# The last store of a rotary-embedding kernel: 128 partitions in one transfer, or 127 and then one in pieces

## The chip, the cores and the metric

The kernel runs on one core of a Trainium2 chip. The metric is device time in microseconds (us) of one execution; the time before is the median of three runs. Engines are named as in the profile: PE is TensorE, DVE is VectorE, ACT is ScalarE, POOL is GpSimd, SP is SyncE. SyncE and ScalarE issue the transfers; 16 DMA engines carry them out.

## The reference

The input is `x` of 16 batches x 512 positions x 1024 values in float32, 32 MiB, seen as 16 heads of 64. `cos` and `sin` are 512 x 32. Each head's two halves are rotated:

```python
x = x.reshape(batch, seq, num_heads, head_dim)
x1, x2 = (x[..., :half_dim].copy(), x[..., half_dim:].copy())
cos = cos[None, :, None, :].copy()
sin = sin[None, :, None, :].copy()
rotated = np.concatenate([x1 * cos - x2 * sin, x1 * sin + x2 * cos], axis=-1)
```

The output has the size of the input, so 32 MiB are read and 32 MiB written at the least.

## The kernel before

**Tiles.** The 16 batches make ten tiles (L41). Batches 0, 1, 14 and 15 are tiles of their own ("singles"): each of 128 partitions holds `R1` = 4 consecutive positions, one run of 4 x 1024 float32 = 16 KB in DRAM and in SBUF. The other twelve batches go in pairs: a partition holds `R2` = 8 consecutive positions of one batch, a run of 32 KB, and the two batches of a pair alternate over the partitions. A position of all 128 partitions is one unit of work `u` (128 x 1024 values); there are `NU` = 64. All tiles live in one ring in SBUF, `x_sb`, of 40 units; the result is written over the input.

**The work of a unit.** `on_vector` multiplies x by cos into PSUM (L332), `on_gpsimd` multiplies the swapped halves by the signed sin (L292; for some units VectorE does it, L325), and the sum is either VectorE's (`comb`, L343) or, for the units of `PE2`, an accumulation on TensorE (L253) that ScalarE copies back to SBUF (L220).

**Loads.** `on_scalar` issues most loads (L155), `on_sync` those of tile 2 and half of tile 0 (L162). The last three loads wait for a store to free their part of the ring (`later`, `sem_out`).

**Stores.** `on_sync` goes through the units; at the last unit of a tile `wait_added` waits until its sums are in SBUF, and one `dma_start` writes the tile. `in_sbuf(t)` gives the tile as 128 partitions x the run of a partition, `in_dram(o1, o2, t)` the same bytes in DRAM. Stores whose space a load needs count on their own semaphore `sem_out[k]`; the rest, among them the last, count on `sem_rest`, each by 16. After the last store SyncE waits until `sem_rest` has counted them all, and the program ends. All stores, in order, are on SyncE's queue (q1 in the profile); ScalarE's is q10.

The last tile is batch 15, a single: 128 rows of 16 KB, 2 MiB.

Of the kernel before, what the change touches and what calls it, by code (L numbers as in the profile page):

```python
# [6 lines left out]
def bass_split_heads_rope_kernel(  # L7
# [22 lines left out]
    R2 = 2 * R1  # L30
# [11 lines left out]
    NT = len(tiles)  # L42
# [3 lines left out]
    NU = len(rows)  # L46
    EARLY = (NU - RING) // R2
# [20 lines left out]
    EH = H * HD // BANK  # L68
    LEAD = 1
    LAG = 14  # L70

    with ExitStack() as stack:
        x_sb = stack.enter_context(nc.sbuf_tensor([P, RING, H, 2, HALF], fp32))
# [13 lines left out]
        sem_rest = stack.enter_context(nc.semaphore("rest"))  # L87
# [22 lines left out]
        o1 = out.rearrange("b (s r) h d -> b s (r h d)", r=R1)  # L110
        x2 = x.rearrange("b (s r) d -> s b (r d)", r=R2)
        o2 = out.rearrange("b (s r) h d -> s b (r h d)", r=R2)
        xs = x_sb[:].rearrange("p n h t d -> p n (h t d)")

        def in_dram(single, pairs, t):
            b, n = tiles[t]
            return single[b] if n == R1 else pairs[:, b:b + 2, :]

        def in_sbuf(t):
            b, n = tiles[t]  # L120
            k = b * R1 % RING
            return x_sb[:, k:k + n].rearrange("p n h t d -> p (n h t d)")

        def where(u):
            t, r = rows[u]
            return t, r, u % RING
# [7 lines left out]
        def wait_added(eng, u):  # L134

            if n_pe[u]:
                eng.wait_ge(sem_a, n_pe[u])
            if n_comb[u]:
                eng.wait_ge(sem_v, n_comb[u])
# [10 lines left out]
        def stores_of(k):  # L150

            return sum(b * R1 // R2 == k for b, _ in tiles)
# [4 lines left out]
        def load_rows(eng, t, lo, hi, sem):  # L157
            w = x.shape[2]
            src = in_dram(x1, x2, t)
            src = src[:, lo * w:hi * w] if tiles[t][1] == R1 else src[:, :, lo * w:hi * w]  # L160
            k = tiles[t][0] * R1 % RING
            eng.dma_start(  # L162
                x_sb[:, k + lo:k + hi].rearrange("p n h t d -> p (n h t d)"), src
            ).then_inc(sem, 16)

        def load_table(eng, i):
            table, sem = ((cos, sem_cos), (sin, sem_sin))[i]
            eng.dma_start(stage[:, i, :], table.rearrange("(s r) d -> s (r d)", r=R1)).then_inc(sem, 16)  # L168
# [9 lines left out]
        def on_sync(sp):  # L178
            load_rows(sp, 0, R1 // 2, R1, sem_in[0])
            load_table(sp, 1)  # L180
            load_rows(sp, 2, 0, R1, sem_in[2])
            load_rows(sp, 2, R1, R2, sem_low)
            for u in range(NU):
                t, r, k = where(u)
                if r == tiles[t][1] - 1:
                    wait_added(sp, u)
                    k = u // R2
                    sp.dma_start(in_dram(o1, o2, t), in_sbuf(t)).then_inc(sem_out[k] if k < EARLY else sem_rest, 16)
            sp.wait_ge(sem_rest, 16 * sum(stores_of(k) for k in range(EARLY, NU // R2)))

        def on_scalar(ae):
            later = {}
            for t, (b, n) in enumerate(tiles):
# [7 lines left out]
                else:  # L201

                    later.setdefault((b * R1 - RING) // R2 * R2 + R2 - 1 + LAG, []).append(t)

# [94 lines left out]
        def on_vector(ve):  # L299
# [50 lines left out]
            for u in range(NU + LEAD):  # L350
                if u < NU:
                    mul(u)
                if u >= LEAD and not PE2[u - LEAD]:
                    comb(u - LEAD)

        on_sync(nc.sync)
        on_scalar(nc.scalar)
        on_gpsimd(nc.gpsimd)
# [35 lines left out]
```

## Time and profile before

| | |
|---|---|
| time, median of three runs | 161.31 us (161.28 to 161.55) |
| the profiled execution: time, span | 161.29 us, 159.9 us |
| granted TensorE clock, mean | 0.795 |
| busy share of the span: DVE, POOL, PE, ACT | 81%, 82%, 40%, 15% |
| DMA packets, bytes, mean rate | 3457, 67.25 MB, 421 GB/s |
| SyncE's queue q1, ScalarE's queue q10, share of 16 engines | 57.0%, 41.5% |
| store of a single, issue to landing, median of four | 23.1 us |
| store of a pair, issue to landing, median of six | 32.2 us |
| the last store, issue and landing | issued at 146.97 us, landed 12.9 us later |

The span runs from the first to the last instruction of the profiled execution. The page cuts it into 40 equal slices; a digit is the busy share of a slice in tenths, for an engine or as a mean over the 16 DMA engines. The DMA view can be asked for any stretch of time; it then cuts that stretch into 40 slices, puts each packet into the slice in which it starts, and counts the packets by size. Here a packet of 16 KB is one partition's row of a single, one of 32 KB is a row of a pair, one of 512 B is a row of a table, and the tiny ones under 512 B are the writes with which an engine reports that its part of a transfer is done. "Share of 16 engines" is the packets' time over 16 times the stretch.

### The profile page before, as it was taken

The numbers are of one execution on the slowest core, as the hardware profiler recorded it, in microseconds if no ns is written. First come the engines' busy times: TensorE is split into PE (matmuls) and PEld (weight loads), VectorE is DVE, ScalarE is ACT, GpSimd is POOL, SyncE is SP. The second block draws the span as 40 slices with busy tenths as digits, with TensorE's granted clock in tenths as the row PEclk, the third lists the DMA queues.
The fourth block names the chain that finished last, engine by engine and source line by source line (L and its number), as shares of the span: only waits on it lengthen the run. The fifth ranks groups of instructions, "written<-read, shape, count | busy, mean of one in ns | idle before, by whom it ended". The sixth has DMA issues, their size and how long they took to land.

```text
span 159.9 us, 503 instructions
## 1 busy us (share of the span) xinstructions
PE 63.9 (40%) x94; PEld 21.6 (14%) x94; DVE 129.5 (81%) x117; ACT 24.4 (15%) x27; POOL 131.5 (82%) x41
## 2 busy tenths in 40 slices
PE   6050008076408640887076407640887075000000
PEld 1020011021102110222021102110222021000000
DVE  0069777999999999998999999999998995497000
ACT  0420001103300430024003300430024005000000
POOL 1069999999999999999999999999999981991000
PEclk9999999999985899557659975899557959855555
DMA  5999999999999999999999999999999999999896
GB/s 137 417 446 435 430 447 476 394 394 418 435 492 426 396 410 443 484 426 402 435 476 402 394 517 394 402 455 394 459 439 467 439 422 443 410 402 492 353 455 275
DMA packets 3457, 67.25 MB, mean 421 GB/s; under 512 B 384, under 2 KB 640, under 8 KB 640
## 3 DMA queue, kind: packets, MB, share of 16 engines
q1 hardware_dynamic: 2016, 38.86, 57.0%
q10 hardware_dynamic: 1440, 28.38, 41.5%
q14 instruction: 1, 0.01, 0.0%
HBM read 33.69 MB, written 33.55 MB: 421 GB/s over the span
## 4 chain that ended last, share of the span: by engine, by line
DMA 55%; DVE 19%; POOL 6%; issue 6%; PE 3%; ACT 1%; ACTq 1%; DVEq 0%; SPq 0%
DMA x_sb<-in_x_dram 34%; DMA out_dram<-x_sb 22%; DVE t_ps L332 9%; DVE x_sb L343 8%; POOL t_sb L292 6%; PE t_ps L253 3%; DVE t_sb L325 2%; ACT x_sb L220 1%; ACTq L168 0%; ACTq L162 0%; ACTq L155 0%; DVE tab_ps L309 0%; DVEq L342 0%; DVE tab_ps L310 0%; DVEq L329 0%
## 5 line engine op out<-in xcount | busy, mean ns | idle before, releaser
L292 POOL TENSOR_TENSOR t_sb<-x_sb,s_sb 128x2048 f32<-128x2048 f32 (+1 forms) x35 | 130.8, 3785 | 12.3 <-ACT s_sb L212 8.2
L253 PE MATMUL t_ps<-t_sb,ident 128*128 128x512 f32 x84 | 59.1, 847 | 63.9 <-DVE t_ps L332 51.6
L332 DVE TENSOR_TENSOR t_ps<-x_sb,pair_ps 128x1024 f32<-128x1024 f32 x48 | 57.5, 1220 | 0.8 <-ACT x_sb L220 0.8
L343 DVE TENSOR_TENSOR x_sb<-t_ps,t_sb 128x1024 f32<-128x1024 f32 x43 | 52.2, 1216 | 4.6 <-POOL t_sb L292 4.4
L220 ACT ACTIVATE x_sb<-t_ps 128x1024 f32<-128x1024 f32 x21 | 21.5, 1023 | 101.9 <-PE t_ps L253 101.9
L253 PEld LDWEIGHTS t_ps<-t_sb,ident 128*128 128x128 f32 x84 | 19.7, 260 | 103.1 <-DVE t_ps L332 74.0
L332 DVE TENSOR_TENSOR t_ps<-x_sb,tab_ps 128x1024 f32<-128x1024 f32 x16 | 19.2, 1222 | 3.0 <-ACT x_sb L220 2.0
L325 DVE TENSOR_TENSOR t_sb<-x_sb,tab_ps 128x1024 f32<-128x1024 f32 x6 | 7.3, 1210 | 0.0
L302 DVE COPY tab_ps<-stage 128x128 f32<-128x128 f32 x1 | 0.3, 294 | 8.0 <-DMA stage<-in_cos_dram 8.0
L237 PE MATMUL pair_ps<-stage,pick 128*128 128x256 f32 x4 | 2.0, 664 | 5.3 <-DMA stage<-in_cos_dram 5.3
L230 PE MATMUL t_ps<-zero 128*128 128x512 bf16 x6 | 2.7, 630 | 1.2 <-DVE zero L300 1.2
L237 PEld LDWEIGHTS pair_ps<-stage,pick 128*128 128x128 f32 x4 | 1.2, 322 | 6.3 <-issue 6.1
L206 ACT ACT_TABLE_LOAD x1 | 1.3, 1283 | 4.2 <-issue 4.2
L230 PEld LDWEIGHTS t_ps<-zero 128*128 128x128 bf16 x6 | 0.7, 138 | 2.3 <-DVE zero L300 1.2
L300 DVE MEMSET zero<- 128x256 uint32 x1 | 0.3, 272 | 0.9 <-PEq L376 0.9
L211 ACT ACTIVATE s_sb<-stage 128x128 f32<-128x128 f32 x1 | 0.3, 309 | 3.0 <-DMA stage<-in_sin_dram 3.0
L215 ACT ACTIVATE s_sb<-pair_ps 128x256 f32<-128x256 f32 x1 | 0.4, 384 | 1.9 <-PE pair_ps L237 1.9
L264 POOL MEMSET ident<- 128x128 f32 x1 | 0.2, 205 | 0.3 <-POOLq L376 0.3
L206 ACT ACTIVATE pick<-ident 128x256 f32<-128x256 f32 x1 | 0.4, 416 | 0.0
L216 ACT ACTIVATE s_sb<-pair_ps 128x256 f32<-128x256 f32 x1 | 0.4, 378 | 0.0
L266 POOL TENSOR_SCALAR_AFFINE_SELECT ident<-ident 128x128 f32<-128x128 f32 x1 | 0.3, 292 | 0.1
L376 POOL MEMSET const-float32-0.0<- 128x1 f32 x1 | 0.1, 98 | 0.3 <-issue 0.3
(6 smaller groups left out, 1.0 us busy)
## 6 DMA issues: line engine op xcount, KB each, us to landing
out_dram<-x_sb SPq DMA_DIRECT2D x6, 4096.0 KB, 32.2
x_sb<-in_x_dram ACTq DMA_DIRECT2D x5, 4096.0 KB, 31.3
out_dram<-x_sb SPq DMA_DIRECT2D x4, 2048.0 KB, 23.1
x_sb<-in_x_dram ACTq DMA_DIRECT2D x3, 2048.0 KB, 22.7
x_sb<-in_x_dram SPq DMA_DIRECT2D x2, 2048.0 KB, 23.9
x_sb<-in_x_dram SPq DMA_DIRECT2D x1, 1024.0 KB, 7.5
x_sb<-in_x_dram ACTq DMA_DIRECT2D x1, 1024.0 KB, 7.9
stage<-in_sin_dram SPq DMA_DIRECT2D x1, 64.0 KB, 7.7
```

Of the source, the lines that this page charges most:

```text
L206: ae.activation(pick[:], ident[:].rearrange("q (s k) -> q k s", k=2)[:, :, :, None].broadcast_to([P, 2, P // 2, 2]), COPY).then_inc(sem_g, 1)
L211: ae.activation(s1_sb[:, :, 0, :], sv, COPY, scale=-1.0)
L215: ae.activation(s2[:, :, :, 0, :], pair_ps[:, :, 1, :, :], COPY, scale=-1.0)
L216: ae.activation(s2[:, :, :, 1, :], pair_ps[:, :, 1, :, :], COPY).then_inc(sem_s, 1)
L220: ae.activation(xs[:, u % RING, :], t1_ps[:, u % NT1, :], COPY).then_inc(sem_a, 1)
L230: pe.matmul(t1_ps[:, k, b * BANK:(b + 1) * BANK], zero[:, 0:P], zero[:], start=True, stop=True).then_inc(sem_w, 1)
L237: pe.matmul(pair_ps[:, k].rearrange("p c r d -> p (c r d)"), pick[:, k].rearrange("q s b -> q (s b)"), stage[:].rearrange("q c f -> q (c f)"),
L253: ins = pe.matmul(t1_ps[:, u % NT1, b * BANK:(b + 1) * BANK], ident[:], t2[:, b * BANK:(b + 1) * BANK], start=False, stop=True, skip_group ...
L292: pl.tensor_tensor(t2_sb[:, u % NT2:u % NT2 + n], x_sb[:, k:k + n, :, ::-1, :], table[:, :, None, :, :].broadcast_to([P, n, H, 2, HALF]), ...
L325: ve.tensor_tensor(t2_sb[:, u % NT2, :, :, :], swapped(k), over_heads(v_ps), mult)
L332: ve.tensor_tensor(t1_ps[:, u % NT1, :].rearrange("p (h d) -> p h d", d=HALF), x_sb[:, k, :, :, :].rearrange("p h t d -> p (h t) d"), c_of ...
L343: ve.tensor_tensor(xs[:, k, :], t1_ps[:, u % NT1, :], t2_sb[:, u % NT2, :, :, :].rearrange("p h t d -> p (h t d)"), add,).then_inc(sem_v, 1)
```

## The change

The last tile's store is taken out of the common line and goes through a new function `store_last`, still on SyncE's queue and at the same place in its order. It issues three transfers: partitions 0 to 126 as they were, and partition 127, whose run of 16 KB is seen as 32 pieces of 512 bytes, in two transfers of 16 pieces each (the even pieces, then the odd ones). All three count on `sem_rest`, so the last wait asks for 32 more. No other store, load or computation is touched.

```diff
+    WHOLE = 127
+    PIECE = 128
...
                     k = u // R2
+                    if t == NT - 1:
+                        store_last(sp, t)
+                        continue
                     sp.dma_start(in_dram(o1, o2, t), in_sbuf(t)).then_inc(sem_out[k] if k < EARLY else sem_rest, 16)
-            sp.wait_ge(sem_rest, 16 * sum(stores_of(k) for k in range(EARLY, NU // R2)))
+            sp.wait_ge(sem_rest, 16 * (2 + sum(stores_of(k) for k in range(EARLY, NU // R2))))
+
+        def store_last(sp, t):
+
+            dst, src = in_dram(o1, o2, t), in_sbuf(t)
+            sp.dma_start(dst[:WHOLE], src[:WHOLE]).then_inc(sem_rest, 16)
+            for i in range(2):
+                piece = [a[WHOLE:].rearrange("p (q i e) -> p q i e", i=2, e=PIECE)[:, :, i, :] for a in (dst, src)]
+                sp.dma_start(*piece).then_inc(sem_rest, 16)
```

## The prediction

> **What bounds the kernel now.** I read the page's slices and queue list first, then the chain, SyncE's waits, the DMA issues, and last the DMA view over short windows at the end. The page and its DMA part:
>
> ```profile
> span 159.9 us, 503 instructions
> ...
> DMA  5999999999999999999999999999999999999896
> GB/s 137 417 446 435 430 447 476 394 394 418 435 492 426 396 410 443 484 426 402 435 476 402 394 517 394 402 455 394 459 439 467 439 422 443 410 402 492 353 455 275
> DMA packets 3457, 67.25 MB, mean 421 GB/s; under 512 B 384, under 2 KB 640, under 8 KB 640
> ...
> q1 hardware_dynamic: 2016, 38.86, 57.0%
> q10 hardware_dynamic: 1440, 28.38, 41.5%
> ...
> DMA 55%; DVE 19%; POOL 6%; issue 6%; PE 3%; ACT 1%; ACTq 1%; DVEq 0%; SPq 0%
> ```
>
> The 16 DMA engines are busy in every slice but the first and the last ones: 57.0 + 41.5 = 98.5% of the span, and DMA holds 55% of the chain. VectorE (81%) and GpSimd (82%) have slack. SyncE's waits, and its last issue in the timeline:
>
> ```profile
> SPq L189 <- DMA out_dram<-x_sb: 12.5, 1, 12.5
> ...
> 146.97 0.34 SPq L188 DMA_DIRECT2D out_dram<-x_sb  x1
> ```
>
> The last store is issued at 146.97 and nothing follows but a wait of 12.5 us for data: no engine computes after 147 us. So the end is set by how fast the DMA engines drain what is queued, and the changed transfer is the last of it. Three windows of the DMA view, 153.70 to 158.70, 153.76 to 154.65 and 158.62 to 159.9 us:
>
> ```profile
> DMA packets 150, 2.11 MB, mean 423 GB/s; under 512 B 21, under 2 KB 21, under 8 KB 21
> ...
> GB/s 1473 737 1473 737 736 2210 0 737 736 0 736 736 0 737 0 0 0 0 0 0 0 0 0 0 0 0 736 736 736 2209 0 1473 736 1473 0 1473 0 736 0 737
> DMA packets 46, 0.49 MB, mean 552 GB/s; under 512 B 16, under 2 KB 16, under 8 KB 16
> ...
> GB/s 0 0 0 0 0 0 0 0 512 0 0 0 0 0 0 0 0 0 0 0 0 0 0 0 0 0 0 0 0 0 0 0 0 0 0 0 0 0 0 0
> DMA packets 17, 0.02 MB, mean 13 GB/s; under 512 B 16, under 2 KB 16, under 8 KB 16
> ...
> q1 hardware_dynamic: 17, 0.02, 3.7%
> ```
>
> Packets are put where they start. A packet of the last store is one partition's row of 16 KB. In the second window the 16 tiny packets are the completions of the store before, one for each engine, so the engines pass to the last store between 153.77 and 154.64 us, most by 154.1 (the starts ahead of the gap). In the third, one engine is late: its eighth and last row starts at 158.89 (slice 8 of 0.032 us), when every other engine has started its last row before 158.62, and ends near 159.5; the span ends 0.4 us after that.
>
> **The price of a row.** The late engine's first row starts at 154.64 and its eighth at 158.89: 4.25 us for seven, 0.607 us a row, or 27.0 GB/s. The mean over the whole run gives 0.985 x 16 x 159.9 us = 2520 engine-us for 67.24 MB, so 0.614 us for 16 KB. That late row runs when the others are finished: the third window's 3.7% of 16 x 1.28 us is 0.76 us, less 16 completions of about 0.01 us each leaves 0.61. A row costs the same beside fifteen busy engines and beside none.
>
> **How a transfer is dealt.** The DMA view lists 24 issues (10 stores, 14 loads), and the page has 384 packets under 512 B: 16 completions for each, so each ran on 16 engines, in equal shares (128 rows, 8 each, in the last). Every one of the 24 fills or empties 128 partitions, which sixteen divides. 127 has no such share: it is prime, and the only equal share on at most 16 engines is all of it on one. The trace shows no transfer with a remainder, so this is bounded from both sides: one engine moves 127 rows, or the rows go 8 to fifteen engines and 7 to the last. I take one engine, because equal shares are what all 24 rows show and an uneven deal is what none shows.
>
> [...]
>
> **The sum.** Everything up to 146.97 us is unchanged: same instructions, same queues.
> - Two more issues on SyncE, 0.34 us each by the row above, so 0.7 us, up to 1.2 at the longest store issue (0.63). They end before 148.7; the first row of the last store starts at 153.77. The older stores' backlog of 6.8 us covers them: nothing. Without a backlog they would cost those 0.7 to 1.2 us. Behind the waiting instruction on SyncE is only the end.
> - Removed: 8 rows on each of 16 engines, 4.86 us.
> - Added: 127 rows one after another on one engine, 127 x 0.607 = 77.1 us (78.0 at 0.614). They begin when that engine is through with the store before: 153.77 to 154.64, and 153.9 is taken since most engines start near it.
> - The last partition: two transfers of 16 pieces, one of 512 B for each engine in each. Window 7 to 9 us has the 256 table packets of that size: its 35.4 engine-us, less 0.75 MB of rows at 27.0 GB/s and 64 completions, leave about 0.03 us for one. On the loaded engine two pieces and their completions add 0.07 us behind the 127 rows; the bound above is a whole row's time each, 1.2 us, the bound below zero. On the other fifteen engines they are done before 155 us and hidden.
> - The wait now counts 32 more and ends with the last piece: 0.4 us to the span's end, as before.
>
> 153.9 + 77.1 + 0.07 + 0.4 = 231.5 us of span. The profiled execution took 161.29 us for a span of 159.9, so 1.4 lies around it; 161.29 is within 0.02 of the median 161.31. That gives **232.9 us**, 71.6 us or 44% more than before. Ends: 153.77 + 77.1 + 0 + 0.4 + 1.4 = 232.7 and 154.64 + 78.0 + 1.2 + 0.4 + 1.4 = 235.6. A long run on a lone engine is shown by a single row only, so I leave 1% of the 77 us (0.8) either way: 231.9 to 236.4.
>
> **Rivals.**
> - *The 127 rows are dealt unevenly, and nothing is lost* (the other side). Place: the late engine of the third window. If it is the one that gets 7 rows, it ends 0.61 us sooner, and the next latest sets the end: the window from 159.1 to 159.3 holds one other completion, so that one ends around 159.2. Gain 0.3, less 0.07 for pieces: about 161.1. If another engine gets the 7, the late one also carries the pieces: 161.4. It decides if a remainder is allowed at all. For it: 16 completions fit it as well. Against: no transfer shows unequal shares. Chance 0.04, inside 0.2% except in a corner. (0.2%, 0.32 us, is about what a measurement of this kernel can tell; its three runs span 0.27.)
> - *The lone engine runs faster*, because 431 GB/s is a limit that all sixteen share. At twice the speed: 153.9 + 38.6 + 0.47 + 1.4 = 194.4. For it: the queues run at 421 to 440 GB/s through loads and stores alike, like a common ceiling. Against: the lone row of 0.61 us. Chance 0.03. [...] The trace's engines moved 27.0 in either condition, so the sum keeps 0.607.
> - *The lone engine runs slower*, each row waiting for the last to land. The 0.4 us between the last row's end and the span's end is a bound for landing: 127 x 0.4 = 51 us more, 283.7. Against: the eight rows of the late engine followed at 0.607 us, no longer than one of them lasts, so rows already overlap their landing. Chance 0.03.
> - That the transfers cover something else than the whole tile: 127 rows and 2 x 16 x 512 B (the other 16 KB) make all 128, so no.
>
> **The numbers.** Forecast 0.90, with a predicted time of 232.9 and a range of 231.2 to 236.6: the bounds above, and 0.2 to 0.7 us for scatter. It leaves the three rivals out, 0.10 together. Slower by over 0.2%: 0.90 + 0.03 + 0.03 = 0.96; within: 0.03; faster: 0.01.
>
> **What would show it.** In the page after, the slices on the right read 0 to 1 in DMA and near 27 GB/s over a third of the span, the span is near 231.5, the mean near 290 GB/s (67.25 MB over it). SyncE's last wait grows from 12.5 to about 83 us. The last wait's window holds 127 rows at 0.607 us each with no two at once, and packets under 512 B number 384 + 1 + 32 - 16 = 401 if the 127 end in one completion; 416 would say sixteen engines. The prediction is wrong if the store's rows are still spread (span near 160), or if rows of the lone engine start at other than 0.61 us apart.

## The result, and the profile after

The changed kernel takes 233.00 us (median of four runs, 232.96 to 233.12) against 161.30 us: a ratio of 1.444, interval 1.4416 to 1.4466. The prediction was 232.9. The profiled execution took 233.12 us for a span of 231.7.

The page after, the lines that answer to those of before:

```profile
span 231.7 us, 505 instructions
...
DMA  6999999999999999998999999950000000000000
GB/s 216 437 427 436 427 430 444 458 413 412 450 441 441 402 436 447 447 441 385 447 430 427 438 430 441 413 246 25 28 25 28 25 31 25 28 28 25 28 25 23
DMA packets 3505, 67.25 MB, mean 290 GB/s; under 512 B 401, under 2 KB 689, under 8 KB 689
```

Up to slice 26 (of 5.8 us) the engines are about as busy as before. From there to the end, a third of the span, the 16 DMA engines together move 23 to 31 GB/s: one engine's worth, 16 KB in 0.607 us being 27.0. The packets under 512 B are 401: 23 older transfers with 16 completions, 32 for the two transfers of pieces, and one for the 127 rows.

Two windows of the DMA view of the kernel after, 153.70 to 155.00 and 155 to 225 us:

```profile
GB/s 0 0 0 0 504 0 504 0 504 504 0 0 0 0 0 0 0 0 0 0 0 0 0 504 0 0 0 0 0 0 0 0 0 0 0 0 0 0 0 0
...
DMA packets 176, 1.92 MB, mean 27 GB/s; under 512 B 30, under 2 KB 60, under 8 KB 60
```

In the first (slices of 0.0325 us) the last start stands alone in slice 23, at 154.46: the lone engine's second row. The first one started 0.607 us before that, at 153.86, in slice 4; the other starts are last rows of the store before, on other engines. In the second window, 176 packets less 30 completions and 30 pieces are 116 rows in 70 us, 0.598 to 0.609 us each as one row more or less falls inside. The last of the 127 starts at 230.35 us, 126 rows after the first: 0.607 us each.

SyncE did not go as predicted. Its waits, its part of the timeline from 140 us, and the two issues of line 202 (the pieces) by themselves; in the last line the columns are the shortest, median and longest duration in ns, and the starts of the first and last:

```profile
SPq L194 <- DMA out_dram<-x_sb: 42.1, 1, 42.1
...
147.14 0.31 SPq L199 DMA_DIRECT2D out_dram<-x_sb  x1
147.50 42.04 SPq L202 DMA_DIRECT2D out_dram<-x_sb  x2
...
L202 SPq DMA_DIRECT2D out_dram<-x_sb x2: 3003/20995/38987, 147.5 to 186.5; - x2
```

The 127 rows were issued in 0.31 us. The first transfer of pieces then held SyncE for 39.0 us, the second for 3.0, and only after them came the wait, 42.1 us. Where the 512 B went, in the windows 187.1 to 187.6 and 190.1 to 190.7 us:

```profile
DMA packets 31, 0.02 MB, mean 48 GB/s; under 512 B 15, under 2 KB 30, under 8 KB 30
...
DMA packets 31, 0.02 MB, mean 40 GB/s; under 512 B 15, under 2 KB 30, under 8 KB 30
```

Fifteen pieces and their completions each, at 187 and 190 us instead of before 155, and one row of the lone engine beside them. The sixteenth piece of each is the lone engine's, after its rows.

### The profile page after: what moved, and what is told of

The parts are those of the page before. It is cut to its first block, busy times and chain, and to the rows that moved or that the text cites. A ratio compares the mean times of both kernels' runs of the same rounds, so it can differ in the third digit from the quotient of the medians.

```text
span 231.7 us, 505 instructions
## 1 busy us (share of the span) xinstructions
PE 66.8 (29%) x94; PEld 22.8 (10%) x94; DVE 129.6 (56%) x117; ACT 24.4 (11%) x27; POOL 131.5 (57%) x41
## 4 chain that ended last, share of the span: by engine, by line
DMA 38%; DVE 12%; POOL 4%; issue 4%; PE 3%; ACT 1%; ACTq 1%; DVEq 0%; SPq 0%
DMA x_sb<-in_x_dram 24%; DMA out_dram<-x_sb 15%; DVE t_ps L345 6%; DVE x_sb L356 5%; POOL t_sb L305 4%; PE t_ps L266 3%; DVE t_sb L338 1%; ACT x_sb L233 1%; ACTq L170 0%; ACTq L164 0%; ACTq L157 0%; DVE tab_ps L322 0%; DVEq L355 0%; DVE tab_ps L323 0%; DVEq L342 0%
## 5 line engine op out<-in xcount | busy, mean ns | idle before, releaser
L266 PE MATMUL t_ps<-t_sb,ident 128*128 128x512 f32 x84 | 62.0, 890 | 62.9 <-DVE t_ps L345 50.5
L266 PEld LDWEIGHTS t_ps<-t_sb,ident 128*128 128x128 f32 x84 | 20.9, 275 | 103.7 <-DVE t_ps L345 73.4
```

The costliest lines, as they stand in the source:

```text
L266: ins = pe.matmul(t1_ps[:, u % NT1, b * BANK:(b + 1) * BANK], ident[:], t2[:, b * BANK:(b + 1) * BANK], start=False, stop=True, skip_group ...
```

## Experiments

**1. Is the late issue of the pieces on the path?** The pieces go first.

```diff
+            for i in range(2):
+                ...
+                sp.dma_start(*piece).then_inc(sem_rest, 16)
             sp.dma_start(dst[:WHOLE], src[:WHOLE]).then_inc(sem_rest, 16)
-            for i in range(2):
-                ...
```

> Same three transfers, the two of pieces issued ahead of the 127 rows. Theory (the end is one engine's 127 rows, everything else is hidden): the pieces run on all engines near 154 us, SyncE is not held for 42 us, and the time stays at 233.0 (232.7 to 233.3). Rival (SyncE held by the full queue of the loaded engine is itself on the path, or the late pieces are): the time falls, at the most by the 3 us that SyncE spent on the second piece transfer, to 230.0.

Measured: 232.68 us (232.53 to 233.04), ratio to before 1.439 (1.430 to 1.448), which takes in the 1.444 of the change. SyncE's waits and the timeline from 140 us:

```profile
SPq L194 <- DMA out_dram<-x_sb: 81.0, 1, 81.0
...
147.38 1.93 SPq L201 DMA_DIRECT2D out_dram<-x_sb  x2
149.35 0.83 SPq L202 DMA_DIRECT2D out_dram<-x_sb  x1
```

The 42 us became waiting and nothing ended 3 us sooner: holding SyncE cost no time, because nothing that mattered was queued behind it. What was held in the change, for 39.0 and 3.0 us, was issued behind the long transfer; with the long one last, all three issues had ended by 150.2 us.

**2. Is the limit the queue or the engine?** The 127 rows go out on ScalarE's queue, after ScalarE has waited for the same sums; the pieces stay on SyncE's.

```diff
-            sp.dma_start(dst[:WHOLE], src[:WHOLE]).then_inc(sem_rest, 16)
...
+            wait_added(ae, NU - 1)
+            dst, src = in_dram(o1, o2, NT - 1), in_sbuf(NT - 1)
+            ae.dma_start(dst[:WHOLE], src[:WHOLE]).then_inc(sem_rest, 16)
```

> The 127 rows are issued on ScalarE's queue, which is empty by then; the pieces stay on SyncE's. Theory (the engine is the limit, not the queue): the rows can start at 147.5 but share their engine with the rest of the store before, its total work is the same, and the time stays at 233.0 (232.7 to 233.4); the pieces run by 155 us. Rival (a queue is the limit, and the second queue runs beside the first): the 127 rows start 6.4 us sooner at full speed and the time is about 226.6.

Measured: 232.69 us (232.57 to 232.78). In the window 147 to 153.5 us of the DMA view the two queues are:

```profile
q1 hardware_dynamic: 157, 2.62, 94.0%
q10 hardware_dynamic: 3, 0.05, 1.8%
```

Three of the 127 rows moved before 153.5, 0.62 us each (1.8% of 16 x 6.5 us), and the time is still 0.3 us from the change's 233.00. So the older store's rows on the same engine are taken to have come as much later; here another queue was no other engine.

**3. Do two such transfers take two engines?** The tile goes out as 61 and 67 partitions.

```diff
-            sp.dma_start(dst[:WHOLE], src[:WHOLE]).then_inc(sem_rest, 16)
-            for i in range(2):
-                ...
+            for lo, hi in [(0, 61), (61, 128)]:
+                sp.dma_start(dst[lo:hi], src[lo:hi]).then_inc(sem_rest, 16)
```

> No pieces; the last store goes out as 61 and 67 partitions in two transfers, both prime. Theory (equal shares, and a transfer with one share always uses the same engine): 128 rows in turn on one engine, 153.9 + 128 x 0.607 + 0.4 + 1.4 = 233.4. Rival (each transfer takes another engine): the 67 rows set the end, 153.9 + 67 x 0.607 + 0.4 + 1.4 = 196.4.

Measured: 233.22 us (two runs, 233.19 and 233.25). The page's count of packets, and the DMA view from 155 to 230 us:

```profile
DMA packets 3443, 67.25 MB, mean 290 GB/s; under 512 B 370, under 2 KB 626, under 8 KB 626
...
DMA packets 125, 2.02 MB, mean 27 GB/s; under 512 B 2, under 2 KB 2, under 8 KB 2
```

370 = 23 x 16 + 2: one completion each. The two followed one another at 27 GB/s, one engine's rate, so both are read as one engine's.

**4. Does every queue deal so?** The 127 rows are issued by GpSimd, after its last multiplication and the same wait, on a semaphore of their own.

```diff
-            sp.dma_start(dst[:WHOLE], src[:WHOLE]).then_inc(sem_rest, 16)
...
+            wait_added(pl, NU - 1)
+            dst, src = in_dram(o1, o2, NT - 1), in_sbuf(NT - 1)
+            pl.dma_start(dst[:WHOLE], src[:WHOLE]).then_inc(sem_l, 16)
```

> The 127 rows are issued by GpSimd on its own queue, with a semaphore of their own; the pieces stay on SyncE's queue. Theory in its wide form (every queue deals in equal shares): 233.0. Rival (it is the queues of SyncE and ScalarE alone that deal so; GpSimd's deals 8 rows to fifteen engines and 7 to the last): 161 to 162.5, the upper end where GpSimd's own issue outlasts the 6.8 us of older rows that cover it. [...]

Measured: 165.52 us (165.05 to 165.99), ratio 1.023 (1.017 to 1.029). From 154.7 to 158 us:

```profile
q0 software_dynamic: 51, 0.84, 70.1%
q1 hardware_dynamic: 42, 0.27, 27.2%
```

GpSimd's queue moved 0.84 MB in 3.3 us, 255 GB/s: more than nine engines' worth of 27. 127 rows on more than one engine cannot be equal shares, so the deal was uneven on this queue. But the time is 3 us above the 161 to 162.5 that was expected: 70.1% of 16 x 3.3 us for 51 rows is 0.73 us a row on the mean, not 0.61.

**5 and 6. Is it the largest divisor?** 126 = 14 x 9 and 119 = 7 x 17.

```diff
-            sp.dma_start(dst[:WHOLE], src[:WHOLE]).then_inc(sem_rest, 16)
+            for lo, hi in [(0, 126)]:              # 6: [(0, 119), (120, 128)]
+                sp.dma_start(dst[lo:hi], src[lo:hi]).then_inc(sem_rest, 16)
+            for p in range(126, 128):              # 6: range(119, 120)
             ...                                    # each p in pieces, as in the change
```

> 126 partitions in one transfer, partitions 126 and 127 in pieces of 512 B (four transfers). Theory (equal shares by the largest divisor up to 16): 126 = 14 x 9, so 14 engines move 9 rows, one more than before, two move none: 0.61 us more plus 0.14 for four pieces on each engine, 162.0 if the late engine is among the 14. If the late engine is one of the two that are spared, the next latest sets the end: 161.7. Rival (any size without sixteen as a divisor falls to one engine): 153.9 + 126 x 0.607 + 0.14 + 0.4 + 1.4 = 232.3. Rival (uneven shares of 7 and 8): 161.3 to 161.5.

> 119 partitions in one transfer, partitions 120 to 127 as a second, partition 119 in pieces. Theory: 119 = 7 x 17, so seven engines move 17 rows, and 8 = 8 x 1 puts one more on each of eight: 18 rows on the loaded ones, 153.9 + 18 x 0.607 + 0.07 + 0.4 + 1.4 = 166.7. If the eight rows went to the other engines: 166.1. Rival (one engine): 153.9 + 119 x 0.607 + 1.8 = 227.9 and more. Rival (uneven): 161.3 to 162.

Measured: 165.51 us (165.43 to 165.54) with 126, ratio 1.026 (1.024 to 1.027); 172.57 us (171.41 to 173.86) with 119, ratio 1.070 (1.065 to 1.074). The pages' packet counts, 126 first:

```profile
DMA packets 3581, 67.25 MB, mean 410 GB/s; under 512 B 446, under 2 KB 766, under 8 KB 766
...
DMA packets 3519, 67.25 MB, mean 394 GB/s; under 512 B 415, under 2 KB 703, under 8 KB 703
```

446 = 368 for the older transfers + 64 for four transfers of pieces + **14**; 415 = 368 + 32 + **7** + **8**. By the completions, SyncE's queue gave 128 partitions 16 engines, 127, 61 and 67 one, 126 fourteen, 119 seven and 8 eight: each time the largest divisor of the count up to 16. The direction of the times follows, their size does not: 3.5 and 5.9 us more than the rows were counted at.

**7 and 8. Only rows per engine?** 112 partitions, then 15 and pieces (7), or then 16 (8).

```diff
-            sp.dma_start(dst[:WHOLE], src[:WHOLE]).then_inc(sem_rest, 16)
+            for lo, hi in [(0, 112), (112, 127)]:  # 8: [(0, 112), (112, 128)], no pieces
+                sp.dma_start(dst[lo:hi], src[lo:hi]).then_inc(sem_rest, 16)
```

> 112 partitions in one transfer (7 rows on each of 16 engines), 15 partitions in a second (one row on each of 15), the last partition in pieces as in the change. This is the deal of 8 rows to fifteen engines and 7 to the last, which the change was thought to give under the rival of the prediction. If the engine left out is the late one: 161.0 to 161.2 (0.2 us less than before). If another is the late one: 161.4. Either way within 0.2% of before, or nearly.

> 112 and 16 partitions in two transfers, no pieces: 7 rows and 1 row on each of 16 engines, as many as before, and one more issue. Theory (issues are hidden by the older rows, only rows per engine count): 161.3, the same as before. Rival (each further transfer costs its issue at the end): 161.6 to 162.

Measured: 164.84 us (164.07 to 166.48) and 164.18 us (163.16 to 165.28), ratios 1.023 (1.019 to 1.027) and 1.017 (1.014 to 1.021). Both expectations fell. The shares are the ones that were meant: the page of number 7 counts 431 packets under 512 B, which is 368 + 32 + 16 + 15, and that of number 8 counts 400, which is 368 + 16 + 16. In number 8 every engine has eight rows, as before, and the end is 2.9 us later. The DMA view from 154.7 to 158 us, of before and of number 8:

```profile
DMA packets 81, 1.33 MB, mean 402 GB/s; under 512 B 0, under 2 KB 0, under 8 KB 0
...
q1 hardware_dynamic: 81, 1.33, 93.7%
```

```profile
DMA packets 81, 1.29 MB, mean 392 GB/s; under 512 B 2, under 2 KB 2, under 8 KB 2
...
q1 hardware_dynamic: 81, 1.29, 101.3%
```

Before: 93.7% of 52.8 engine-us over 81 rows, 0.611 us each. Number 8: 101.3% over 79 rows, 0.68 us each. The same arithmetic gives 0.65 for number 7 and 0.64 for number 5. But eight rows of 0.68 instead of 0.61 us make 0.6 us, not 2.9: the mean does not say on which engine the slow rows fall. Three windows of 0.01 us of number 8, from 154.466, 155.325 and 156.565 us, hold the start of one row each:

```profile
q1 hardware_dynamic: 1, 0.02, 535.0%
...
q1 hardware_dynamic: 1, 0.02, 771.2%
...
q1 hardware_dynamic: 1, 0.02, 1009.4%
```

Of 0.16 engine-us these are rows of 0.86, 1.23 and 1.62 us. Each starts where the one before it ends, so they are read as one engine's, and its other five rows follow until about 161.3 us, later than any other engine's. In the kernel before, the late engine ended near 159.5. The difference is 1.8 us, and the profiled run took 1.9 us longer (163.16 against 161.29). So a few rows got much slower, and the end went by the engine that had the three of 0.86, 1.23 and 1.62 us. Whether this is the price of a second transfer or of the deal, 9 and 10 tell apart.

**9 and 10. A second transfer, or the deal?** Halves of each partition's run, or halves of the partitions.

```diff
-            sp.dma_start(dst[:WHOLE], src[:WHOLE]).then_inc(sem_rest, 16)
-            ...
+            for i in range(2):                     # 9
+                half = [a[:, i * 2 * H * HD:(i + 1) * 2 * H * HD] for a in (dst, src)]
+                sp.dma_start(*half).then_inc(sem_rest, 16)
+            for lo, hi in [(0, 64), (64, 128)]:    # 10, instead
+                sp.dma_start(dst[lo:hi], src[lo:hi]).then_inc(sem_rest, 16)
```

> The last store in two transfers of 128 partitions x 8 KB (the halves of each partition's run), no pieces. It tells apart why 112 + 16 partitions took 164.2 us where 161.3 was expected. Theory (rows are slower where the deal over the engines does not keep each engine to partitions of its own, which only 128 partitions do; a further transfer costs nothing): 161.3 to 161.6, the 8 KB packets at half of 0.61 us. Rival (a second transfer at the end costs about 2.9 us, whatever its shape): 164.2.

> The last store as partitions 0 to 63 and 64 to 127, 4 + 4 rows on each of 16 engines. [...] Rival (only shares that are no power of two collide): 161.3 to 161.6. Rival (a second transfer costs 2.9): 164.2. [...]

Measured: 161.34 us (161.28 to 161.63) with halves of the runs, ratio 0.999 (0.997 to 1.001); 165.10 us (165.04 to 165.16) with halves of the partitions, ratio 1.022 (1.017 to 1.026). From 154.7 to 157.7 us in number 10:

```profile
DMA packets 65, 0.87 MB, mean 289 GB/s; under 512 B 12, under 2 KB 12, under 8 KB 12
...
q1 hardware_dynamic: 65, 0.87, 97.1%
```

The second transfer of all 128 partitions cost nothing: 161.34 against 161.39 us. Two of 64 neighbouring partitions, with the same eight rows for each engine (36 completions from 154 to 164 us, as in number 9), cost 3.7 us: 97.1% of 48 engine-us over 53 rows is 0.88 us a row on the mean. The same view for 159.72 to 159.80 and for 158.10 to 158.26 us shows what the mean is made of:

```profile
q1 hardware_dynamic: 4, 0.07, 399.1%
...
q1 hardware_dynamic: 2, 0.03, 47.7%
```

The first four rows took 1.28 us each (399.1% of 16 x 0.08 us, over four), about twice 0.61; the two of the other window took 0.61. Number 9, at a ratio of 0.999, speaks against the second transfer as such, so what is left, as the author's reading, is which partitions, and with them which DRAM addresses, the engines work on together. The author's estimate, that every row would take twice 0.607 us (8 rows, 4.9 us more, 166.2 in all), did not hold: some rows took 1.28 us and others 0.61. Why those rows were slow, and whether the partitions or the DRAM addresses decide it, no run here shows.

## Why the prediction was right, and where it was not

- **The deal** (equal shares, so one engine): right. One completion for the 127 rows, and in the experiments 15, 14, 8, 7 and 1 where the largest divisor said so. No transfer of the kernel before had a remainder, so its trace alone left the choice open, and the 0.04 for the uneven deal was the author's estimate.
- **The row**: 0.607 us forecast for 127 in turn, 116 counted in 70 us. The lone engine was neither faster (rival: 194.4 us) nor slower (283.7).
- **The start**: 153.9 taken because most engines start near it, 153.86 measured. Nothing said that the lone engine would not be the late one, at 154.64, so up to 0.8 us of the close hit is luck.
- **The end**: the sum gave a span of 231.5 and the page says 231.7. The lone engine's two pieces start by 231.02, and the span ends 0.7 us after that, where 0.4 was taken. The 1.4 us around the span held (233.12 - 231.7).
- **The two more issues, "they end before 148.7"**: wrong. They took 42.0 us, because the first of them was held for 39.0. The pieces on the other fifteen engines, "done before 155 us", came at 187 and 190, and SyncE's last wait was 42.1 us, not about 83. None of it moved the end, as experiment 1 shows: the step was wrong in its place and right in its price of nothing.
- **The uneven deal as a rival**, 161.1 to 161.4: it did not happen on SyncE's queue. Where a deal was uneven (GpSimd's), the sum for it was too low as well: it priced rows at 0.61 us whoever moves them, and they took 0.73 on the mean in that window. Experiment 7 is that deal by hand on SyncE's queue, at 164.8 instead of 161.0 to 161.4.
- In experiments 5 and 6 slower rows were not counted. In 5 the end is one engine's: after 159.9 us the view holds 0.07 MB, four rows, moved one at a time. In 6 the profiled run took 172.02 us, 5.3 more than was counted. A row took 0.76 us on the mean from 154.7 us on, and 18 of those instead of 0.607 make only 2.7 us. But the end went by the slowest engine: the last row of all starts at 169.2 us, and 18 rows from 153.9 to its end near 169.8 take 0.88 us each, which makes 5.0.

## What to carry to other kernels

Before a transfer is cut by partitions, work out how many engines the remaining count gives (the completions in the packet count show it: 16, 15, 14, 8, 7 or 1 here on SyncE's queue), and take its rows per engine at the 0.61 us measured here for 16 KB as a first price. The end went by the slowest engine (one row of 1.62 us in number 8, where the mean was 0.68), so the mean row says too little. Cutting along the run instead kept all 128 partitions and cost nothing (161.34 against 161.39 us). And the 127 rows on one engine held SyncE, which issued the next transfer, for 39.0 us, so look at what stands behind it in the issue order.

## What the hardware showed that was not expected

The lone engine's backlog reached back to the issuer. The 127 rows were issued in 0.31 us, yet the next transfer's issue ended only at 186.5 us: (186.5 - 153.86) / 0.607 = 54 rows had been moved and 73 were left. The second was held 3.0 us more, the time of five rows. In experiment 3, with 61 rows issued and then 67, both issues ended within 1.2 us: 61 rows in front held nothing, 127 did. Where between them the holding begins, no run here shows.

Rows of the same 16 KB, eight to an engine, took 0.611 us on the mean when all 128 partitions went in one transfer, 0.68 with 112 and 16, and 0.88 with 64 and 64. The last two means are mixtures: beside rows of 0.61 us stand single ones of 1.62 us in the first and of 1.28 us in the second.
